# Summing activations inside the store to DRAM: a fused encoder layer on one core

## The chip, the cores and the metric

The kernel runs on one core of a Trainium2 chip. Its engines are called by their short names in the profile: PE (TensorE, the matmuls), DVE (VectorE), ACT (ScalarE), POOL (GpSimd) and SP (SyncE, which here only issues transfers). The metric is the time of one execution on the device in microseconds (us). Each engine works through its own list of instructions in order; what one needs from another it gets through semaphores.

## The reference, cut to what matters

One layer of a streaming encoder for 1056 tokens (1024 of a prompt and 32 of a sample), width 1024, hidden width 2816. After a mixing part (attention and a gated recurrence) come a feed-forward block with a short convolution and a last gated product:

```
hf = rms_norm(x, g_pre_ffn)
a, u = split(hf @ w_up, 2)                  # 1024 -> 2 x 2816
ac = b_conv + sum_j ap[:, j:j+t] * w_conv[j]        # causal, 3 taps
ffn = (gelu(ac) * u) @ w_down               # 2816 -> 1024
x = x + rms_norm(ffn, g_post_ffn)
x = x + (pe @ w_ple) * sigmoid(x @ w_ple_gate)
```

Everything is float32. The kernel multiplies each operand as a high and a low part, three PE products for one.

## The kernel before, in words

Only the last 850 us of the program matter here. They hold three stages.

**The up stage** (about 1200 to 1690 us) walks over 22 units `u`, each 128 columns of the hidden width. A unit is seven block products of Strassen's kind (`mults`, L1616 to L1618, 168 matmuls), whose results stand in three PSUM tiles X, Y, Z and are taken out by `after` (for example L1634, `nU3 = Y - s1c`, which must be done before product 5 may write into Y). Weights for the seven products are prepared some products ahead: POOL forms sums of weight blocks (L1431, L1432, L1433, L1438), ACT casts the high part (L1424), DVE subtracts for the low part (L1425). The unit's tail, `ff_tail`, runs while PE is in the next unit: convolution on ACT and DVE (L1533 to L1535), gelu on ACT (L1536), and the product with `u` on DVE (L1540, L1541), which writes the finished hidden activations `out` into one of two halves of the page `Up`.

**The down product** is again seven products `i`, over sums of activations. An even unit and the odd unit after it give the two row halves; each `out` has two column halves. With B11, B12 the halves of the even unit and B21, B22 those of the odd one, `down_parts` stores seven operands into the DRAM tiles `td[0]` to `td[6]`: B11, B11+B22, B21-B11, B22, B21+B22, B11+B12, B12-B22. Before the change the five sums are computed on chip: B11+B12 on POOL after the even unit (L1559), then after the odd unit B11+B22 on DVE (L1565), and B21-B11, B21+B22, B12-B22 on POOL (L1567, L1572, L1575; the last two are asked for by `kept["more"]` during the next unit). SP stores all seven (L1550), 264 KB each. The sums lie in the tiles `a` and `ab` of the convolution, which are free by then.

**The down stage** (about 1686 to 1932 us) reads them back: `x_in` loads a page of `td[i]` (L1708), `x_parts` splits it into high and low part (ACT L1699, DVE L1700), `w_in_` and `w_parts` load and combine w_down (L1728, L1735, L1699, L1700). For each of the seven products `i` there are 12 steps `s` (4 column blocks, each in 3 pieces of the hidden width), 24 or 18 matmuls a step (L1896 to L1898). SP issues all loads in one list. Activations for product i+1 are loaded and split during product i. `d_out` adds results into accumulators (L1767), `square` sums squares of finished ones (L1796 on ACT, L1797 on DVE).

For the norm of the first column half, `x2_norm(0)` is called in product 5: it sets a small tile `nv` to one (L1804), sums the squares over partitions with 12 one-column matmuls (L1807), and DVE makes the inverse root in 12 tiny instructions (L1808, L213 to L219). `x2_rows(0)` turns the result into rows with 12 small transposes on PE (L303). `x2_part` then applies the norm. **The gate stage** (from about 1932 us) is the last product, 2 halves `h` by 8 blocks `c` (L1987 to L1989); during half 0 the norm of the second half is made in the same way (`x2_norm(1)`, `x2_rows(1)`).

What sets the order: the program is written in the order above, but instructions that wait for nothing in the program may be put earlier in their engine's list by the scheduler that builds it. `with behind(E)` forbids that: what stands in it comes after the engine's latest instruction so far. SP and POOL each have one list, and an instruction that waits holds up all behind it there.

## Time and profile before

| | |
|---|---|
| time, median of 3 runs | 2048.68 us (2040.51 to 2050.8) |
| time of the profiled execution | 2047.88 us |
| its span, first to last instruction | 2045.9 us |
| mean granted TensorE clock | 0.989 |
| PE busy | 1987.5 us, 97% |
| DVE busy | 1498.2 us, 73% |
| ACT busy | 963.7 us, 47% |
| POOL busy | 300.9 us, 15% |

A row of the group view reads: line, engine, operation, tiles out<-in, shapes, number | busy us, mean ns of one | idle us of the engine just ahead of them and what ended it. A row of the stage view reads: stretch, its length, then for each engine busy us and in brackets the number of instructions, then the granted PE clock, the busy share of the DMA engines and GB/s. A row of the timeline has start, duration (us), engine, line and instruction; in square brackets the idle time before it and who ended it. A row of the waits has who waited, for whom, total us, times, longest. Matmuls overlap one another, so the time that PE needs is better counted in matmuls than in busy time: an undisturbed stretch of 50 us holds 416.

### The profile page before, as it was taken

The page shows a single profiled execution, that of the slowest core. Times are in us where ns is not written, and L with a number is a line of the kernel's source. Part 1 is how long each engine was busy: PE and PEld are TensorE (multiplying, and loading weights), DVE is VectorE, ACT ScalarE, POOL GpSimd, SP SyncE. Part 2 cuts the span into 40 slices and gives each one's busy share as a digit, 9 for nine tenths or more (in the row PEclk, how much of TensorE's full clock was granted, in tenths as well). Part 3 has the DMA queues.
Part 4 walks back from the last instruction along what each step waited for, and adds up shares of the span by engine and source line. Part 5 has one row for each costly group of instructions (what it writes and reads, how often), then busy time and mean ns, then how long its engine had stood idle before and what let it go on. Part 6 is the DMA issues. An engine that isn't in the chain of part 4 may idle for free. (4 is left out here: it accounts for less than half of the span.)

```text
span 2045.9 us, 38767 instructions
## 1 busy us (share of the span) xinstructions
PE 1987.5 (97%) x14858; PEld 1953.8 (95%) x14858; DVE 1498.2 (73%) x3194; ACT 963.7 (47%) x2206; POOL 300.9 (15%) x373
## 2 busy tenths in 40 slices
PE   7999999999999999999999989999999999998998
PEld 6999999999999999999999989999999998998998
DVE  6788888688888888353553868888888896777752
ACT  6555566566666666441224743333333344443432
POOL 2110100000000000012000114444554521000000
PEclk9999999999999999999999989999999999998999
DMA  8322311411111111486653552323233258897433
GB/s 261 100 88 80 110 54 61 138 42 57 57 56 56 40 53 54 137 256 188 201 163 94 179 159 79 100 86 102 81 105 100 84 175 250 241 274 228 138 108 85
DMA packets 315537, 251.71 MB, mean 123 GB/s; under 512 B 14344, under 2 KB 300571, under 8 KB 315352
## 3 DMA queue, kind: packets, MB, share of 16 engines
q1 hardware_dynamic: 308402, 227.01, 37.0%
q0 software_dynamic: 6880, 22.17, 3.2%
q8 instruction: 116, 1.90, 0.4%
q14 instruction: 69, 0.57, 0.1%
q10 hardware_dynamic: 70, 0.06, 0.0%
HBM read 180.71 MB, written 68.47 MB: 122 GB/s over the span
## 5 line engine op out<-in xcount | busy, mean ns | idle before, releaser
L1616 PE MATMUL st<-op,wt 128*128 128x264 f32 x1232 | 352.7, 286 | 19.4 <-DVE Sp L1634 16.4
L1618 PE MATMUL st<-op,wt 128*128 128x264 f32 x1232 | 351.2, 285 | 0.0
L1617 PE MATMUL st<-op,wt 128*128 128x264 f32 x1232 | 349.6, 284 | 0.0
L1616 PEld LDWEIGHTS st<-op,wt 128*128 128x128 f32 x1232 | 233.2, 189 | 24.1 <-DVE Sp L1634 20.7
L1617 PEld LDWEIGHTS st<-op,wt 128*128 128x128 f32 x1232 | 233.1, 189 | 0.0
L1618 PEld LDWEIGHTS st<-op,wt 128*128 128x128 f32 x1232 | 232.6, 189 | 0.0
L1424 ACT CAST wt<-wu 128x512 fp32r<-128x512 f32 x132 | 80.5, 619 | 210.8 <-POOL wu L1433 91.1
L1898 PE MATMUL st<-X,wd 128*128 128x264 f32 x616 | 177.6, 288 | 2.1 <-DVE wd L1700 2.1
L1896 PE MATMUL st<-X,wd 128*128 128x264 f32 x616 | 177.2, 288 | 2.4 <-ACT wd L1699 2.4
L1897 PE MATMUL st<-X,wd 128*128 128x264 f32 x616 | 176.8, 287 | 0.0
L202 PE MATMUL mm<-La,wh 128*128 128x384 f32 (+1 forms) x504 | 166.5, 331 | 0.3 <-ACT kt L342 0.3
L203 PE MATMUL mm<-Lb,wh 128*128 128x384 f32 (+1 forms) x504 | 162.5, 322 | 0.0
L204 PE MATMUL mm<-La,wl 128*128 128x384 f32 (+1 forms) x504 | 162.5, 322 | 0.0
L204 PE MATMUL mm<-Ra,wl 128*128 128x264 f32 x512 | 145.1, 284 | 1.2 <-DVE wl L186 1.2
L202 PE MATMUL mm<-Ra,wh 128*128 128x264 f32 x512 | 145.5, 284 | 0.0
L203 PE MATMUL mm<-Rb,wh 128*128 128x264 f32 x512 | 145.0, 283 | 0.0
L1425 DVE TENSOR_TENSOR wt<-wu,wt 128x512 fp32r<-128x512 f32 x132 | 116.4, 882 | 36.3 <-ACT wt L1424 36.2
L1896 PEld LDWEIGHTS st<-X,wd 128*128 128x128 f32 x616 | 118.7, 193 | 2.6 <-ACT wd L1699 2.6
L1898 PEld LDWEIGHTS st<-X,wd 128*128 128x128 f32 x616 | 118.6, 192 | 2.5 <-DVE wd L1700 2.5
L1897 PEld LDWEIGHTS st<-X,wd 128*128 128x128 f32 x616 | 118.6, 193 | 0.0
L186 DVE TENSOR_TENSOR wl<-wr,wh 128x1024 fp32r<-128x1024 f32 x64 | 78.2, 1223 | 54.8 <-ACT wh L183 53.4
L455 ACT ACTIVATE sc<-sc,st 128x257 f32<-128x257 f32 (+1 forms) x144 | 69.7, 485 | 74.9 <-DVE st L450 73.8
(468 smaller groups left out, 6056.3 us busy)
## 6 DMA issues: line engine op xcount, KB each, us to landing
wq<-in_w_down_dram SPq DMA_DIRECT2D x96, 256.0 KB
wu<-in_w_up_dram SPq DMA_DIRECT2D x44, 512.0 KB
wu<-in_w_in_dram SPq DMA_DIRECT2D x32, 512.0 KB
X<-td SPq DMA_DIRECT2D x28, 528.0 KB
wr<-in_w_in_dram SPq DMA_DIRECT2D x26, 512.0 KB
wq<-in_w_down_dram SPq DMA_DIRECT2D x48, 192.0 KB
td<-a SPq DMA_DIRECT2D x33, 264.0 KB
wr<-in_w_out_dram SPq DMA_DIRECT2D x16, 512.0 KB
```

The source lines that it names most:

```text
L186: V.tensor_tensor(lo[:], raw[:], hi[:].bitcast(F32), op=ALU.subtract)
L202: E.matmul(ps, wh, a, start=first and n == 0, stop=False)
L203: E.matmul(ps, wh, b, start=False, stop=False)
L204: E.matmul(ps, wl, a, start=False, stop=last and n == len(ks) - 1)
L1424: S.copy(t[:, 0], src)
L1425: V.tensor_tensor(t[:, 1], src, t[:, 0].bitcast(F32), op=ALU.subtract)
L1616: E.matmul(o, wh, xh, start=first and k == 0, stop=False, skip_group_check=True)
L1617: E.matmul(o, wh, xl, start=False, stop=False, skip_group_check=True)
L1618: E.matmul(o, wl, xh, start=False, stop=k == 3, skip_group_check=True)
L1896: E.matmul(o, w[:, 0, k, :], x[:, 0, k, :], start=first, stop=False)
L1897: E.matmul(o, w[:, 0, k, :], x[:, 1, k, :], start=False, stop=False)
L1898: E.matmul(o, w[:, 1, k, :], x[:, 0, k, :], start=False, stop=last)
```

## The change: what it does

Three edits.

**The sums are made by the transfers.** `down_parts` computes no sum any more. SP stores one term of each operand plainly (`to_td`), and POOL issues a transfer that adds the other term to what lies in DRAM (`add_td`, `accum_op=ALU.add`). Terms with a minus are negated by ACT first (`S.mul(neg, ..., -1.0)`, into the front of the tile `a`). For a pair of units that makes 7 plain stores from SP as before, 5 adding transfers from POOL of 264 KB each (11 pairs: 55), and 2 negations on ACT (22 in all). Gone are 44 additions on POOL and 11 on DVE. `kept["more"]` is gone with them, and the tile `ab` is no longer used for sums.

**The norm's scratch.** The memset of `nv` is held behind DVE's latest instruction.

**The column sums come later.** `x2_norm(0)` moves from step 2 to step 4 of product 5, `x2_rows(0)` from step 4 to step 8; for the second half `x2_norm(1)` moves from block 0 to block 1, `x2_rows(1)` from block 1 to 2 and the parts from blocks 2 to 5 to blocks 3 to 6.

```diff
-    def to_td(issue, i, k, src):
-        issue(td[i][k // 4][:, :, k % 4, :], src)
+    def to_td(i, k, src):
+        dma(td[i][k // 4][:, :, k % 4, :], src)
+
+    def add_td(i, k, src):
+        gdma(td[i][k // 4][:, :, k % 4, :], src, accum_op=ALU.add)
 
     def down_parts(f, a, ab, out):
 
         k, o4 = f // 2, halves(out)
-        a2 = a[:, 0:T].rearrange("p (b a c) -> p b a c", b=2, a=2)
-        b2 = ab[:, 0:T].rearrange("p (b a c) -> p b a c", b=2, a=2)
+        neg = a[:, 0:T].rearrange("p (b a c) -> p b a c", b=2, a=2)[:, 0]
+        b1, b2 = o4[:, :, 0, :], o4[:, :, 1, :]
         if f % 2 == 0:
-            to_td(dma, 0, k, o4[:, :, 0, :])
-            G.tensor_tensor(a2[:, 0], o4[:, :, 0, :], o4[:, :, 1, :], op=ALU.add)
-            to_td(dma, 5, k, a2[:, 0])
-            kept["even"] = o4
+            S.mul(neg, b1, -1.0)
+            to_td(0, k, b1)
+            to_td(1, k, b1)
+            to_td(2, k, neg)
+            to_td(5, k, b1)
+            to_td(6, k, b2)
+            add_td(5, k, b2)
             return
-        e4 = kept.pop("even")
-        to_td(dma, 3, k, o4[:, :, 1, :])
-        V.tensor_tensor(a2[:, 0], e4[:, :, 0, :], o4[:, :, 1, :], op=ALU.add)
-        to_td(dma, 1, k, a2[:, 0])
-        G.tensor_tensor(b2[:, 0], o4[:, :, 0, :], e4[:, :, 0, :], op=ALU.subtract)
-        to_td(dma, 2, k, b2[:, 0])
-
-        def more_sums(n):
-            if n == 0:
-                G.tensor_tensor(a2[:, 1], o4[:, :, 0, :], o4[:, :, 1, :], op=ALU.add)
-                to_td(dma, 4, k, a2[:, 1])
-            else:
-                G.tensor_tensor(b2[:, 1], e4[:, :, 1, :], o4[:, :, 1, :], op=ALU.subtract)
-                to_td(dma, 6, k, b2[:, 1])
-        kept["more"] = more_sums
+        S.mul(neg, b2, -1.0)
+        to_td(3, k, b2)
+        to_td(4, k, b2)
+        add_td(1, k, b2)
+        add_td(2, k, b1)
+        add_td(4, k, b1)
+        add_td(6, k, neg)
...
     def x2_norm(h):
...
-        V.memset(v[:], 1.0)
+        with behind(V):
+            V.memset(v[:], 1.0)
...
-                if i == 5 and s == 2:
+                if i == 5 and s == 4:
                     x2_norm(0)
-                if i == 5 and s == 4:
+                if i == 5 and s == 8:
                     with behind(E):
                         x2_rows(0)
...
                 if c == 0:
-                    x2_norm(1)
                     x2_load(1, 0)
                 if c == 1:
+                    x2_norm(1)
+                if c == 2:
                     with behind(E):
                         x2_rows(1)
-                if 1 < c < 6:
-                    for k in (2 * c - 4, 2 * c - 3):
+                if 2 < c < 7:
+                    for k in (2 * c - 6, 2 * c - 5):
```

How the instructions stand now. First DVE in the up stage, where the tail of an odd unit falls into the next unit: `Up` is the page of the finished activations, `Sp` the scratch that L1634 (L1632 in the changed kernel) writes, `wt` prepared weights. Before:

```order
L1540 TENSOR_TENSOR Up_15230<-a_17298,Up_15230 128x1024
L1541 TENSOR_TENSOR Up_15230<-a_17298,Up_15230 128x32
L1565 TENSOR_TENSOR a_17298<-Up_15230 128x528
L1631 TENSOR_TENSOR ab_17316<-st_17313,rbT 128x2x264
L1425 TENSOR_TENSOR wt_17499<-wu_17322,wt_17499 128x512
L1634 TENSOR_TENSOR Sp_14920<-st_17314,Sp_14920 128x528
```

and now:

```order
L1540 TENSOR_TENSOR Up_15230<-a_17310,Up_15230 128x1024
L1541 TENSOR_TENSOR Up_15230<-a_17310,Up_15230 128x32
L1629 TENSOR_TENSOR ab_17330<-st_17327,rbT 128x2x264
L1425 TENSOR_TENSOR wt_17509<-wu_17336,wt_17509 128x512
L1632 TENSOR_TENSOR Sp_14920<-st_17328,Sp_14920 128x528
```

The sum of B11 and B22 is gone; the rest keeps its order. At the same place ACT had the gelu (L1536) and three casts of the next weights:

```order
L1424 CAST wt_17471<-wu_17322 128x512
L1536 ACTIVATE a_17298<-a_17298 128x1058
L1424 CAST wt_17499<-wu_17322 128x512
L1424 CAST wt_17550<-wu_17324 128x512
L1424 CAST wt_17582<-sa_17439 128x512
```

and has now

```order
L1424 CAST wt_17481<-wu_17336 128x512
L1536 ACTIVATE a_17310<-a_17310 128x1058
L1569 ACTIVATE a_17310<-Up_15230 128x528
L1424 CAST wt_17509<-wu_17336 128x512
L1424 CAST wt_17564<-wu_17338 128x512
```

The negation (L1569, L1561 after an even unit) stands between the gelu and the casts, and reads `Up`, so it waits for DVE's L1541. POOL, from the tail of an odd unit to that of the next even one (`td_1_145` is a tile of `td[2]`, `_142` of `td[1]`, `_157` of `td[6]`, `_151` of `td[4]`, `_154` of `td[5]`), has now

```order
L1553 DMA td_1_145<-Up_15230 256x1x264
L1553 DMA td_1_142<-Up_15230 256x1x264
L1553 DMA td_1_157<-a_17310 256x1x264
L1438 TENSOR_TENSOR wu_17336<-wu_17336 128x512
L1553 DMA td_1_151<-Up_15230 256x1x264
L1431 TENSOR_TENSOR sa_17680<-wu_17569 128x512
L1432 TENSOR_TENSOR wu_17569<-wu_17567,wu_17569 128x512
L1433 TENSOR_TENSOR wu_17567<-wu_17567,sa_17680 128x512
L1599 MEMSET ab_17792 128x2
L1600 COPY ab_17792<-cach 128x2
L1438 TENSOR_TENSOR wu_17567<-wu_17567 128x512
L1553 DMA td_1_154<-Up_15230 256x1x264
```

where before the three sums L1567, L1572 and L1575 stood ahead of L1438 after the odd unit and L1559 after the even one. Three adding transfers come ahead of the weight sum L1438, one behind it, and after an even unit the one transfer comes behind L1438.

Third, DVE at the norm of the first column half in product 5 of the down stage, from the last split ahead of it (`nv`, `rsb`, `rst`, `nr` are the tiles of the inverse root, `wd` and `wq` weights, `X` activations of product 6). Before:

```order
L1700 TENSOR_TENSOR wd_22194<-wq_22077,wd_22194 128x512
L1700 TENSOR_TENSOR X_22157<-X_22157 128x1056
L1808 TENSOR_SCALAR nv_22132<-tr_22131 88x6
L1767 TENSOR_TENSOR acc_20092<-acc_20092,st_22037 128x528
L213 TENSOR_SCALAR rsb_22142<-nv_22132 128x6
L1700 TENSOR_TENSOR wd_22240<-wq_22110,wd_22240 128x384
L214 TENSOR_SCALAR rsb_22142<-rsb_22142 128x6
L1735 TENSOR_TENSOR wq_22163<-wq_22163 128x512
L217 SCALAR_TENSOR_TENSOR rst_22143<-rsb_22142 128x6
L1735 TENSOR_TENSOR wq_22198<-wq_22198 128x512
L218 TENSOR_TENSOR rst_22143<-rst_22143,nv_22132 128x6
L1700 TENSOR_TENSOR X_22192<-X_22192 128x792
```

and now:

```order
L1694 TENSOR_TENSOR X_22249<-X_22249 128x792
L1729 TENSOR_TENSOR wq_22255<-wq_22255 128x384
L1803 TENSOR_SCALAR nv_22226<-tr_22225 88x6
L213 TENSOR_SCALAR rsb_22236<-nv_22226 128x6
L214 TENSOR_SCALAR rsb_22236<-rsb_22236 128x6
L1694 TENSOR_TENSOR wd_22312<-wq_22196,wd_22312 128x512
L217 SCALAR_TENSOR_TENSOR rst_22237<-rsb_22236 128x6
L218 TENSOR_TENSOR rst_22237<-rst_22237,nv_22226 128x6
L219 SCALAR_TENSOR_TENSOR nr_22227<-rst_22237,rsb_22236 128x6
L217 SCALAR_TENSOR_TENSOR rst_22237<-nr_22227 128x6
L218 TENSOR_TENSOR rst_22237<-rst_22237,nv_22226 128x6
L219 SCALAR_TENSOR_TENSOR nr_22227<-rst_22237,nr_22227 128x6
```

The norm's instructions stood among the splits and now come nearly in one piece, behind the last split of activations for product 6 (`X_22249`). On PE the column sums stand 48 products later than before, and between them and the rows lie 84 products instead of 62. Both memsets of `nv` (L1804) stood early in the down stage, during product 0; now each stands by its norm.

More of the change, by code (lines that the diff above doesn't have):

```diff
@@ L1681, in up_unit @@
                     after(a, ps)
-                if n == 1 and "more" in kept:
-                    kept["more"](0)
-                if n == 2 and "more" in kept:
-                    kept.pop("more")(1)
                 if u == NF - 1:
@@ L1876, in layer_kernel @@
                     finish_up()
-                    for a in range(2):
-                        kept["more"](a)
                     fctx.close()
```

## The prediction

> **What bounds the kernel now.** I read the totals first, then the table by stage, to see in which stages PE stands still, then the waits of PE there, and last the timeline around each wait.
>
> ```profile
> PE 1987.5 (97%) x14858; PEld 1953.8 (95%) x14858; DVE 1498.2 (73%) x3194; ACT 963.7 (47%) x2206; POOL 300.9 (15%) x373
> 1300.00:1350.00 50.00, 48.42 (x398) 48.03 (x397) 41.41 (x52) 17.12 (x29) 23.78 (x18) 1.00 0.34 102
> 1700.00:1750.00 50.00, 45.51 (x359) 44.88 (x358) 31.29 (x47) 20.37 (x32) 9.96 (x3) 0.97 0.86 251
> 1800.00:1850.00 50.00, 50.00 (x416) 50.00 (x415) 37.48 (x55) 22.50 (x34) 0.00 (x0) 1.00 0.89 260
> 1850.00:1900.00 50.00, 43.79 (x314) 43.38 (x313) 37.08 (x65) 18.61 (x29) 0.00 (x0) 0.86 0.69 208
> PE st L1616 <- DVE Sp L1634: 14.2, 9, 1.6
> ...
> L1616 PE MATMUL st<-op,wt 128*128 128x264 f32 x1232 | 352.7, 286 | 19.4 <-DVE Sp L1634 16.4
> L1616 PEld LDWEIGHTS st<-op,wt 128*128 128x128 f32 x1232 | 233.2, 189 | 24.1 <-DVE Sp L1634 20.7
> ```
>
> PE bounds the program, so a change gains only what it takes out of PE's standstills. An undisturbed 50 us (1800 to 1850) holds 416 matmuls, 0.120 us each. The start of the down stage (1700 to 1750) holds 57 fewer: 6.9 us lost. Product 5 with its norm (1850 to 1900) holds 102 fewer: 12.3 us. In the up stage PE waited 9 times, 14.2 us in all, for L1634. These three places are those that the change touches.
>
> **The up stage: the sum that goes.** The tail of an odd unit against that of the even unit before it:
>
> ```profile
> 1419.44 1.23 DVE L1540 TENSOR_TENSOR Up<-a,Up 128x1024 f32<-128x1024 f32 x1 [0.29 <-ACT a L1536]
> 1421.30 1.48 DVE L1425 TENSOR_TENSOR wt<-wu,wt 128x512 fp32r<-128x512 f32 x1
> 1422.70 0.69 DVE L1634 TENSOR_TENSOR Sp<-st,Sp 128x528 f32<-128x528 f32 x1
> 1423.45 0.39 PE L1616 MATMUL st<-op,wt 128*128 128x264 f32 x1
> ...
> 1440.04 1.23 DVE L1540 TENSOR_TENSOR Up<-a,Up 128x1024 f32<-128x1024 f32 x1 [0.29 <-ACT a L1536]
> 1441.18 0.19 DVE L1541 TENSOR_TENSOR Up<-a,Up 128x32 f32<-128x32 f32 x1
> 1441.41 1.84 DVE L1565 TENSOR_TENSOR a<-Up 128x528 f32<-128x528 f32 x1
> 1444.90 0.70 DVE L1634 TENSOR_TENSOR Sp<-st,Sp 128x528 f32<-128x528 f32 x1
> 1445.65 0.39 PE L1616 MATMUL st<-op,wt 128*128 128x264 f32 x1 [1.58 <-DVE Sp L1634]
> ```
>
> From the start of L1540 to that of L1634 the even unit takes 3.26 us, the odd one 4.86, and only the odd one makes PE wait, 1.58 us. But in the even one too the matmul starts 0.06 us after L1634 ends (1423.39): there is no slack, and whatever else delays L1634 costs PE as much.
>
> In the changed kernel L1565 is gone, and the cast of the next weights stands behind the negation on ACT. Its price, and that of what lies around it:
>
> ```profile
> L1796 ACT ACTIVATE sq<-acc 128x528 f32<-128x528 f32 x14 | 8.9, 645 | 11.7 <-DVE acc L1767 11.6
> 1439.91 0.60 ACT L1424 CAST wt<-wu 128x512 fp32r<-128x512 f32 x1
> 1418.45 0.69 DVE L1425 TENSOR_TENSOR wt<-wu,wt 128x512 fp32r<-128x512 f32 x1 [1.22 <-ACT wt L1424]
> ```
>
> After L1540 begins, the page is ready at 1.33 us (end of L1541), the negation takes 0.65 (the nearest ACT pass over 528 columns), the cast 0.60, L1425 0.69 when POOL computes nothing beside it: L1634 starts at 3.27 us, in both kinds of unit. For odd units that is 1.59 us sooner, all of the 1.58 us wait; for even ones 0.01 us later, no change. POOL's next sum, L1438, waits for that L1425 and cannot run beside it. So the 9 waits go: 14.2 us. Bounds: if the tails of even units become shorter too, at most the 4.3 us that PE's weight loads waited beyond the matmuls come on top (20.7 against 16.4 in the last two rows of the first fence); if ACT starts its negation later by a few tenths in each of 20 units, each tenth costs 2 us. I take 14.0, nearest the rows.
>
> **What the adding transfers cost.** The trace holds none; bounds from the plain ones that POOL issues:
>
> ```profile
> L1213 POOL DMA_DIRECT2D mx_d<-ta x32 | 17.3, 542 | 593.4 <-DVE ta L1212 593.2
> L1403 POOL DMA_DIRECT2D ple_d<-ple x8 | 6.1, 756 | 25.6 <-ACT ple L1401 19.8 <-issue 5.7
> mx_d<-ta POOLq DMA_DIRECT2D x32, 132.0 KB, 3.3
> ple_d<-ple POOLq DMA_DIRECT2D x8, 528.0 KB, 6.3
> ```
>
> 264 KB lies between: 0.54 to 0.76 us of POOL, 3.3 to 6.3 us to land, more if reading the target counts. Three issues (about 1.9 us) replace three sums (at least 1.3 us each) ahead of L1438, so POOL is sooner than now; the fourth waits for a store to land, behind L1438, when POOL has nothing to do before the next L1431. Nothing reads a sum before the down stage, and an `Up` half is rewritten some 25 us after it is finished. So I take nothing for them here; the upper bound is the first rival. [...]
>
> **The start of the down stage.**
>
> ```profile
> 1699.87 7.53 POOL L1567 TENSOR_TENSOR ab<-Up 128x528 f32<-128x528 f32 x1 [21.55 <-DMA wq<-in_w_down_dram]
> 1697.33 1.26 SPq L1728 DMA_DIRECT2D wq<-in_w_down_dram  x1
> SPq L1550 <- POOL ab L1567: 6.9, 1, 6.9
> 1711.29 0.56 SPq L1728 DMA_DIRECT2D wq<-in_w_down_dram  x1
> 1714.26 0.10 DVE L1804 MEMSET nv<- 128x6 f32 x2 [8.06 <-DMA td<-ab]
> 1720.00:1725.00 5.00, 4.28 (x22) 4.06 (x23) 3.91 (x7) 2.86 (x6) 0.00 (x0) 0.70 1.00 247
> ```
>
> The last odd unit's sum on POOL takes 7.53 us beside DVE's splits; SP waits 6.9 us for it with the weight loads of w_down behind; then the memset of `nv`, whose memory was `ab`, holds DVE 8.06 us until the store has landed, with the splits of weights behind it. PE runs dry and its clock falls to 0.70. All three go: no sum, no store from `ab`, no memset here. What is late next is SP's load of activations of product 1, last piece, which needs an added operand: finished page, two issues on POOL, landing, some 5 to 8 us after L1541. Weights are issued ahead of that load, where now SP issues none for 12.7 us (1698.6 to 1711.3), and they are fetched six steps (about 16 us) before their use. I take 6.5 of the 6.9 us; bounds 3 and 6.9.
>
> **The norm in product 5.**
>
> ```profile
> 1864.11 0.70 DVE L1797 TENSOR_TENSOR sqd<-sqd,sq 128x528 f32<-128x528 f32 x1
> 1864.86 1.53 PE L1807 MATMUL tr<-ones,sqd 128*88 128x1 f32 x12 [4.08 <-DVE sqd L1797]
> 1865.00:1870.00 5.00, 5.00 (x29) 5.00 (x30) 4.98 (x8) 3.17 (x4) 0.00 (x0) 0.53 0.87 269
> 1876.62 0.98 DVE L1700 TENSOR_TENSOR X<-X 128x792 fp32r<-128x792 f32 x1
> 1878.80 2.72 PE L303 MATMUL tr<-ident,nr 88*128 88x88 f32 x12 [2.13 <-DVE nr L219]
> 1924.11 0.70 DVE L226 TENSOR_TENSOR x<-acc,x 128x528 fp32r<-128x528 f32 x1
> 1880.00:1885.00 5.00, 5.00 (x25) 5.00 (x25) 3.03 (x5) 0.76 (x2) 0.00 (x0) 0.50 0.63 177
> ```
>
> PE came to the sums at 1860.78 and waited 4.08 us, then 2.13 us for the rows; the clock fell to 0.53 and 0.50 after them. 48 products later is 5.8 us later: 1866.6, and the squares are done at 1864.81. That wait goes, with 1.8 us to spare. The rows come 1.5 us of sums and 84 products (10.1 us) after that, at 1878.2. DVE's root now stands behind the last split for product 6, which ended at 1877.60, perhaps 0.7 sooner without the small instructions ahead of it; then one combination of weights (0.56), one split (0.69), one addition (0.70) and 12 small instructions at 0.2: ready at about 1881. PE waits some 2.9 us again, and with the clock at half for 5 us as in the last row loses 2.5 more. 12.3 less 5.4 makes 6.9 us. Bounds: 12.3, if activations land sooner, and 2, if the applied norm, which DVE finishes at 1924.8 now (last row of L226), 7 us before the gate stage, is what PE, some 9 us earlier there, waits for next.
>
> [...]
>
> **The gate stage.**
>
> ```profile
> 1935.00:1940.00 5.00, 4.49 (x41) 4.30 (x40) 2.78 (x5) 2.35 (x6) 0.00 (x0) 1.00 0.26 76
> ```
>
> The wait of the second column sums, 0.5 us, goes: a block later their squares are done. The parts end a block later (block 6) and have block 7 as cover, 6.5 us; without it each late microsecond would be PE's.
>
> **The sum**: 14.0 + 6.5 + 6.9 + 0.5 = 27.9 us. From the profiled execution's 2047.88 us: 2020 us; that execution is 0.8 us below the median of the runs.
>
> **Rivals.**
>
> *Adding transfers delay the weights (slower).* Place: the loads of `wu`, from which POOL begins its sums.
>
> ```profile
> 1449.80 1.59 SPq L1413 DMA_DIRECT2D wu<-in_w_up_dram  x2
> 1454.72 1.29 POOL L1431 TENSOR_TENSOR sa<-wu 128x512 f32<-128x512 f32 x1 [5.70 <-DMA wu<-in_w_up_dram]
> ```
>
> Here L1431 began as its weights landed, 4.9 us after the issue; from it the chain runs through L1433, a cast, the gelu and L1540 to L1634, which has no slack. One adding transfer runs near each pair of loads. Each microsecond that it delays them costs 20 units 20 us: from 1.4 us on nothing is left of the gain, from 1.9 us the kernel is clearly slower. With 3 us (half of the 6.3 us of the nearest large transfer): 2020 + 60 = 2080. Against it: the DMA engines are busy 0.34 of this stage. Chance 0.08.
>
> *The negation keeps L1634 late.* ACT is in order; 0.5 us later than I worked out in 20 units leaves 14 - 10 = 4 us of the up stage: 2030. For it: no slack at all. Against it: ACT is busy 17 of 50 us. 0.15.
>
> *The later stalls move instead of going.* SP is held by the landing as long as by the sum, and PE waits for the applied norm: 6.5 falls to 0 and 6.9 to 2, 2031. That is also the case that the edits of the norm don't do what they say. 0.12.
>
> **How the numbers follow.** Forecast 2020 (its own range 2012 to 2026) 0.6; the two middle rivals 0.27; slower 0.08; others near no change 0.05. What a measurement can tell from no change is about 0.5%, 10 us: all that ends below 2038 is faster, 0.86; same 0.07; slower 0.07. The range: below, all of 14.2 + 4.3 + 6.9 + 12.3 + 0.5 = 38 us gained, 2010, and 2 for the spread of runs: 2008; above, 2038, which takes in both middle rivals.
>
> **What would show it.** Right: no wait of PE for the successor of L1634 above 0.3 us, about 411 matmuls in 50 us of the up stage (398 and 1.58 us at 0.12); over 400 in the first 50 us of the down stage; no wait at the column sums, one of 2 to 3 us at the rows. Wrong: POOL's weight sums waiting for `wu`, ACT's casts waiting behind the negation, SP waiting for an adding transfer more than 8 us, or PE idle ahead of the gate stage.

## The result: 1.1% faster, some three quarters of the forecast gain, and not by the instruction that was named

The changed kernel takes 2024.06 us at the median against 2046.77 us before on the same chip: a ratio of 0.9894, 95% interval 0.9863 to 0.9926. The forecast was 2020 us, 27.9 us less than before; the ratio gives 21.7 us. Its profiled execution took 2028.1 us (span 2026.1), 19.8 us less than the profiled one before.

The table by stage at the places whose rows the prediction showed, of the changed kernel (after the window: busy us and count of PE, PEld, DVE, ACT, POOL; granted clock, DMA share, GB/s):

```profile
1300.00:1350.00 50.00, 49.78 (x410) 49.57 (x410) 39.53 (x51) 18.21 (x31) 25.92 (x21) 1.00 0.57 130
1700.00:1750.00 50.00, 48.46 (x393) 47.63 (x393) 33.81 (x47) 25.89 (x40) 0.00 (x0) 1.00 0.96 296
1800.00:1850.00 50.00, 48.65 (x397) 48.02 (x396) 33.63 (x51) 18.90 (x29) 0.00 (x0) 1.00 0.82 242
1850.00:1900.00 50.00, 45.28 (x343) 44.86 (x342) 40.30 (x71) 22.36 (x37) 0.00 (x0) 0.90 0.75 218
```

The up stage went from 398 matmuls to 410, the start of the down stage from 359 to 393, product 5 from 314 to 343. The stretch from 1800 to 1850 us, full before at 416, lost 19.

PE's waits for VectorE in the up stage (us in total, times, longest), where L1632 is the former L1634 and L1627 the former L1629:

```profile
PE st L1614 <- DVE Sp L1627: 2.0, 1, 2.0
PE st L1614 <- DVE Sp L1632: 0.2, 1, 0.2
```

The nine waits of 1.6 us are gone. The tail of an odd unit, by the timeline, shows why L1632 is in time, and what it now stands behind:

```profile
1433.66 1.23 DVE L1540 TENSOR_TENSOR Up<-a,Up 128x1024 f32<-128x1024 f32 x1 [0.30 <-ACT a L1536]
1434.80 0.18 DVE L1541 TENSOR_TENSOR Up<-a,Up 128x32 f32<-128x32 f32 x1
1435.08 0.65 ACT L1569 ACTIVATE a<-Up 128x528 f32<-128x528 f32 x1 [1.45 <-DVE Up L1541]
1435.63 1.13 ACT L1424 CAST wt<-wu 128x512 fp32r<-128x512 f32 x2
1436.26 0.69 DVE L1425 TENSOR_TENSOR wt<-wu,wt 128x512 fp32r<-128x512 f32 x1 [0.66 <-ACT wt L1424]
1436.87 0.70 DVE L1632 TENSOR_TENSOR Sp<-st,Sp 128x528 f32<-128x528 f32 x1
```

From L1540 to L1632 are 3.21 us (4.86 before), on the path that the prediction drew: the negation 0.65 us, the cast, L1425 at 0.69.

To set the kernels side by side, PE's matmuls in five stretches of each profiled execution. A matmul is 0.12 us; the stretches are the up stage, the start of the down stage, products 2 to 4, product 5, and product 6 with the gate stage. The last column is the ratio of the times to those of the kernel before.

| kernel | 1250–1650 | 1650–1750 | 1750–1850 | 1850–1900 | 1900–2000 | ratio, 95% |
|---|---|---|---|---|---|---|
| before | 3150 | 755 | 829 | 314 | 828 | 1 |
| changed | 3250 | 804 | 810 | 343 | 835 | 0.9894 (0.9863–0.9926) |
| norm edits only | 3139 | 771 | 828 | 362 | 835 | 0.9974 (0.9956–0.9992) |
| sums only | 3251 | 796 | 753 | 371 | 835 | 0.9923 (0.9901–0.9945) |
| one sum | 3057 | 761 | 819 | 317 | 833 | 1.0071 (1.0048–1.0094) |
| sum on VectorE | 3252 | 811 | 798 | 345 | 835 | 0.9883 (0.9859–0.9908) |
| idle sums on POOL | 2911 | 740 | 828 | 404 | 771 | 1.0119 (1.0087–1.0151) |
| negated twice | 3164 | 775 | 808 | 350 | 835 | 0.9936 (0.9911–0.9961) |
| plain stores | 3260 | 829 | 812 | 351 | 835 | 0.9866 (0.9840–0.9893) |
| norm later | 3264 | 797 | 792 | 421 | 824 | 0.9868 (0.9846–0.9891) |
| and loads spread | 3252 | 800 | 804 | 421 | 805 | 0.9872 (0.9846–0.9897) |
| and piece late | 3249 | 804 | 791 | 416 | 818 | 0.9867 (0.9847–0.9888) |
| and piece on POOL | 3263 | 785 | 800 | 421 | 811 | 0.9886 (0.9870–0.9903) |
| norm later, piece late, sum on VectorE | 3266 | 818 | 796 | 421 | 820 | 0.9836 (0.9814–0.9858) |

Changed against before: +100, +49, -19, +29, +7, together 166 matmuls or 19.9 us, which is the 19.8 of the two executions (at 1250 us they are level, with 8669 matmuls before and 8663 now). A kernel that is early is further along at the same microsecond, so the stretches behind 1750 us compare only roughly between kernels that differ much (the norm of "sums only" lies partly in its third column, that of the idle sums in the fifth). The first 300 us, whose code is the same in all, hold 1862 to 1916 matmuls from one execution to the next, up to 6.5 us, and at 1250 us the executions lie up to 87 matmuls apart: that is why the counts behind 1250 us say more of small effects than the times.

### The profile page after: what moved, and what is told of

Its sections match the earlier page's. It is cut to its first block, busy times and chain, and to the rows that moved or that the text cites. A ratio compares the mean times of both kernels' runs of the same rounds, so it can differ in the third digit from the quotient of the medians.

```text
span 2026.1 us, 38830 instructions
## 1 busy us (share of the span) xinstructions
PE 1988.8 (98%) x14858; PEld 1955.4 (97%) x14858; DVE 1468.4 (72%) x3183; ACT 974.2 (48%) x2228; POOL 284.0 (14%) x384
## 3 DMA queue, kind: packets, MB, share of 16 engines
q0 software_dynamic: 21840, 37.05, 8.6%
## 4 chain that ended last, share of the span: by engine, by line
PE 62%; issue 8%; DMA 8%; DVE 7%; POOL 7%; ACT 3%; SPq 1%; POOLq 0%; DVEq 0%; ACTq 0%
PE mm L202 7%; PE mm L203 7%; PE mm L204 7%; DMA td<-Up 4%; PE st L1891 2%; PE st L1889 2%; PE st L1890 2%; POOL wu L1433 2%; POOL wu L1432 2%; DMA X<-td 2%; PE st L1980 2%; PE st L1982 2%; PE st L1981 2%; PE G L841 2%; PE Y L838 2%
## 5 line engine op out<-in xcount | busy, mean ns | idle before, releaser
L1425 DVE TENSOR_TENSOR wt<-wu,wt 128x512 fp32r<-128x512 f32 x132 | 107.8, 817 | 47.7 <-ACT wt L1424 47.6
L1891 PEld LDWEIGHTS st<-X,wd 128*128 128x128 f32 x616 | 116.9, 190 | 3.0 <-DVE wd L1694 3.0
L1889 PEld LDWEIGHTS st<-X,wd 128*128 128x128 f32 x616 | 117.1, 190 | 1.6 <-ACT wd L1693 1.6
L1890 PEld LDWEIGHTS st<-X,wd 128*128 128x128 f32 x616 | 117.1, 190 | 0.0
```

Source lines behind the costliest of these rows:

```text
L1425: V.tensor_tensor(t[:, 1], src, t[:, 0].bitcast(F32), op=ALU.subtract)
L1889: E.matmul(o, w[:, 0, k, :], x[:, 0, k, :], start=first, stop=False)
L1890: E.matmul(o, w[:, 0, k, :], x[:, 1, k, :], start=False, stop=False)
L1891: E.matmul(o, w[:, 1, k, :], x[:, 0, k, :], start=False, stop=last)
```

## The experiments

### Each half of the change alone

Kernel before, with the norm's edits alone:

```
+        with behind(V): V.memset(v[:], 1.0)
-  i == 5: x2_norm(0) at s == 2, x2_rows(0) at s == 4
+  i == 5: x2_norm(0) at s == 4, x2_rows(0) at s == 8     (and x2_norm(1), x2_rows(1) one block later)
```

> The kernel before with only the three edits of the norm: memset of nv behind VectorE's earlier work, column sums and rows of both halves issued later. My theory (each part acts in its own place): the up stage is as before (398 matmuls in 50 us, PE waits 1.58 us in odd units for L1634), the norm in product 5 gains about 3.5 us as it did in the changed kernel, the memset's stall of 8.06 us of VectorE at 1714 us goes and gives 1 to 3 us, the gate stage 0.5: 5 to 7 us less than before, ratio about 0.997. Rival (the adding transfers are what makes the later places of the norm useful, or SP's blocked queue alone sets the start of the down stage): 0 to 4 us less.

Changed kernel, with those edits undone:

> The changed kernel with the three edits of the norm undone (memset in its old place, column sums and rows early): only the sums go by adding transfers and ScalarE negates. My theory: up stage as in the changed kernel (410 to 413 matmuls in 50 us), start of the down stage about 4 us better than before, norm as before (314 matmuls between the marks that held 343): 16 to 18 us less than before, ratio about 0.992. Rival (the memset's place and the late norm carry the gain after the up stage, and the adding transfers cost as much behind the up stage as they gain): 10 to 13 us less, ratio about 0.994.

Measured: 5.3 us less (0.9974) and 15.7 us less (0.9923). Together 21.0, against 21.7 for the whole change: by the times the two halves add, about as the first theory had it in both. The intervals (1.6 to 9.0 us and 11.2 to 20.2 us) don't exclude the rivals by themselves. By the counts behind 1250 us the halves alone gain 59 and 130 matmuls, 23 more than the two together; 19 of these are the norm in product 5, which gains 48 alone and 29 in the changed kernel. The norm's edits leave the waits in the up stage as they were. At the start of the down stage they bring only 5 matmuls, 0.6 us (446 from 1690 to 1750 us, 441 before), where 1 to 3 us were expected. The other 11 of the second column are missing in the first: this execution is 62 matmuls ahead at 1250 us, so that a stall which the kernel before has at 1653 us falls ahead of 1650 us here. The memset no longer holds VectorE, but SP and PE wait there as before (waits of PE, then of SP, with the norm's edits alone):

```profile
PE st L1897 <- ACT wd L1699: 4.3, 1, 4.3
...
SPq L1550 <- POOL ab L1567: 6.9, 1, 6.9
```

Without the memset's edit, "sums only" loses 33 matmuls between 1650 and 1750 us (796 of the 829 that a full stretch holds), where the kernel before loses 57 from 1700 to 1750 us alone. Its memset waits for nothing, since nothing is stored from `ab` any more. So POOL's late sum, and the store behind it, were the stall that counted there.

### Which sum was it? L1565 on VectorE, or POOL's sums beside it

Kernel before, with L1565 alone gone, POOL's four sums kept:

```
+            to_td(dma, 1, k, o4[:, :, 0, :])                                          (even unit)
-        V.tensor_tensor(a2[:, 0], e4[:, :, 0, :], o4[:, :, 1, :], op=ALU.add)         (odd unit, L1565)
-        to_td(dma, 1, k, a2[:, 0])
+        gdma(td[1][k // 4][:, :, k % 4, :], o4[:, :, 1, :], accum_op=ALU.add)
```

> The kernel before with one sum changed: only VectorE's L1565 goes (product 1's activations: a store in the even unit, one adding transfer in the odd one); POOL keeps its four sums, ScalarE negates nothing. My theory (L1565 ahead of L1634 on VectorE is the whole wait): L1634's wait falls from 14 us to under 1, some 410 matmuls in 50 us, 12 to 14 us less than before: ratio about 0.9935. Rival (POOL's sums beside VectorE's passes also lengthen the chain to L1634): half of it, 6 to 7 us, ratio 0.997, with waits of 0.5 to 1 us left.

Measured: 1.0071, 14.5 us slower than before. Both theories had it faster. PE's waits in the up stage, and one odd tail by the timeline (line numbers as in the kernel before; L1572 and L1575 are two of POOL's sums, L1438 its weight sum):

```profile
PE st L1616 <- DVE Up L1636: 17.0, 10, 1.7
PE st L1616 <- DVE Sp L1629: 8.9, 9, 1.0
PE st L1616 <- DVE Sp L1634: 2.0, 2, 1.4
```

```profile
1442.60 0.69 DVE L1634 TENSOR_TENSOR Sp<-st,Sp 128x528 f32<-128x528 f32 x1
1443.22 4.34 DVE L1425 TENSOR_TENSOR wt<-wu,wt 128x512 fp32r<-128x512 f32 x1
1447.48 0.69 DVE L1636 TENSOR_TENSOR Up<-Sp,st 128x528 f32<-128x528 f32 x1
...
1442.71 1.77 POOL L1572 TENSOR_TENSOR a<-Up 128x528 f32<-128x528 f32 x1
1443.99 1.78 POOL L1575 TENSOR_TENSOR ab<-Up 128x528 f32<-128x528 f32 x1
1445.27 1.72 POOL L1438 TENSOR_TENSOR wu<-wu 128x512 f32<-128x512 f32 x1
```

L1634 is in time now, but the split L1425 behind it takes 4.34 us instead of 0.69: it ends at 1447.56, 0.57 us after the last of POOL's three passes (1446.99), as if it had only then begun. The stall moved from L1634 to the next result that PE needs, L1636, and became longer. This run also puts an adding transfer between POOL's sums, which moves L1572 some 0.6 us later against L1540; how much of the longer stall is owed to that, no run separates.

In the kernel before, L1565 itself stood beside POOL's sums (the prediction's row has it from 1441.41 to 1443.25 us), and so did the split behind it:

```profile
1441.35 1.34 POOL L1567 TENSOR_TENSOR ab<-Up 128x528 f32<-128x528 f32 x1 [2.98 <-DVE Up L1540]
1442.64 1.78 POOL L1572 TENSOR_TENSOR a<-Up 128x528 f32<-128x528 f32 x1
...
1443.79 1.19 DVE L1425 TENSOR_TENSOR wt<-wu,wt 128x512 fp32r<-128x512 f32 x1
```

L1565 ends 0.56 us after POOL's L1567, and L1425 0.56 us after L1572. L1565 takes 1.84 us for work that takes 0.71 alone (next run), L1425 1.19 for 0.69: 1.13 and 0.50 us too long, 1.63 in all. The whole tail is 1.64 us longer than in the next run, which has the same sum on VectorE and none on POOL (4.86 us against 3.22).

Changed kernel, with VectorE's sum back and POOL summing nothing:

```
-            to_td(1, k, b1)
+            kept["b1"] = b1
-        add_td(1, k, b2)
+        V.tensor_tensor(s1, kept.pop("b1"), b2, op=ALU.add)     (s1: the free half of a)
+        to_td(1, k, s1)
```

> The changed kernel with VectorE's sum for product 1 back (L1565's work and a plain store in odd units); POOL still sums nothing, ScalarE still negates. Theory P (after the run with one sum changed: POOL's sums beside VectorE's passes, not L1565, are the wait): the sum takes 0.70 us instead of 1.85 and lies mostly in the 0.66 us that VectorE waits for ScalarE's cast there; waits of PE under 0.2 us a unit, at most 3 us slower than the changed kernel, ratio to before 0.990 to 0.991. Theory L (the prediction: L1565 itself is the wait): 0.7 to 1.6 us in each of 10 odd units, 7 to 15 us slower than the changed kernel, ratio 0.993 to 0.997.

Measured: 0.9883, the same as the changed kernel; 3252 matmuls in the up stage against 3250. An odd tail (L1573 is the sum, L1634 the changed kernel's L1632):

```profile
1432.02 1.22 DVE L1540 TENSOR_TENSOR Up<-a,Up 128x1024 f32<-128x1024 f32 x1 [0.30 <-ACT a L1536]
1433.16 0.18 DVE L1541 TENSOR_TENSOR Up<-a,Up 128x32 f32<-128x32 f32 x1
1433.38 0.71 DVE L1573 TENSOR_TENSOR a<-Up 128x528 f32<-128x528 f32 x1
1434.01 0.70 DVE L1631 TENSOR_TENSOR ab<-st,rbT 128x528 f32<-128x528 f32 x1
1434.63 0.69 DVE L1425 TENSOR_TENSOR wt<-wu,wt 128x512 fp32r<-128x512 f32 x1
1435.24 0.70 DVE L1634 TENSOR_TENSOR Sp<-st,Sp 128x528 f32<-128x528 f32 x1
```

The sum fits into the time in which VectorE waits for ScalarE's cast (0.66 us in the changed kernel). From the start of L1540 to that of L1634 are 3.22 us, with the sum in between (3.21 in the changed kernel): it costs nothing. Theory P holds, theory L, which was the prediction's, does not.

Changed kernel, with POOL computing sums that nothing reads:

```
+            G.tensor_tensor(d2[:, 0], b1, b2, op=ALU.add)       (even; d2 lies in ab)
+        G.tensor_tensor(d2[:, 0], e1, b2, op=ALU.add)           (odd, three of them)
+        G.tensor_tensor(d2[:, 1], b1, e1, op=ALU.add)
+        G.tensor_tensor(d2[:, 0], b1, b2, op=ALU.add)
```

> The changed kernel, and POOL computes sums as in the kernel before (one in even units, three in odd ones), into memory that nothing reads: results, transfers and ScalarE's negations are the changed kernel's. Theory P (POOL's sums beside VectorE's passes are what made PE wait): the waits at the tails of odd units come back, 1.5 to 2.5 us in each of 10 units, VectorE's splits L1425 grow from a mean of 0.82 us to 1.0 or more, 15 us or more slower than the changed kernel, ratio to before 0.997 or above. Theory L (VectorE's own sum was the wait): the same as the changed kernel within 3 us.

Measured: 1.0119, 24 us slower than before and 46 us slower than the changed kernel; 339 matmuls fewer in the up stage. PE's waits there, and one odd tail (L1639 is the changed kernel's L1632, L1632 its copy L1625 on ScalarE):

```profile
PE st L1621 <- ACT Sp L1632: 23.9, 9, 3.9
PE st L1621 <- DVE Sp L1639: 11.3, 10, 1.2
```

```profile
1447.78 1.87 DVE L1425 TENSOR_TENSOR wt<-wu,wt 128x512 fp32r<-128x512 f32 x1 [0.66 <-ACT wt L1424]
1449.57 0.69 DVE L1639 TENSOR_TENSOR Sp<-st,Sp 128x528 f32<-128x528 f32 x1
1450.18 2.67 DVE L1425 TENSOR_TENSOR wt<-wu,wt 128x512 fp32r<-128x512 f32 x1
...
1446.47 1.34 POOL L1575 TENSOR_TENSOR ab<-Up 128x528 f32<-128x528 f32 x1 [2.98 <-DVE Up L1540]
1447.76 1.33 POOL L1574 TENSOR_TENSOR ab<-Up 128x528 f32<-128x528 f32 x1
```

The splits are long again (1.87 and 2.67 us), with nothing changed but POOL's work. The dose is larger than in the kernel before, though: besides 11.3 us for L1639, PE waits 23.9 us for ScalarE's copy, and POOL, whose sums here stand ahead of its transfers and weight sums, waits 41.4 us for `wu` (5.7 in the kernel before). The sign is shown by this run; the size in the kernel before is not, and rests on the rows of its tail above.

### Is there slack behind the negation?

Changed kernel, each negation done twice:

```
             S.mul(neg, b1, -1.0)
+            S.mul(neg, b1, -1.0)          (and the same for b2 in odd units)
```

> The changed kernel with each negation on ScalarE done twice. Theory (no slack: whatever delays the cast behind the negation delays L1632, and PE waits for it): about 0.55 us in each of 21 units, 11 us slower than the changed kernel, ratio to before about 0.995, PE's wait for L1632 near 0.5 us a unit. Rival (a few tenths to half a microsecond of slack are there since the waits are gone): at most 3 us slower, no wait above 0.2 us.

Measured: 0.9936, 8.6 us slower than the changed kernel by the ratios; 86 matmuls fewer in the up stage, 10.3 us. There is no slack to speak of. But the wait shows elsewhere than expected (lines two further on than in the changed kernel: L1629 is its L1627, L1636 its L1634; for L1634, its L1632, PE waits once, 1.7 us):

```profile
PE st L1616 <- DVE Sp L1629: 7.9, 8, 1.0
PE st L1616 <- DVE Up L1636: 2.0, 9, 0.3
```

VectorE's chain is late as a whole, and PE pays at whichever result comes last.

### What adding costs in the transfer

Changed kernel, with `accum_op` left out of POOL's transfers, so that the second term overwrites the first and the sums are left out:

> The changed kernel with plain stores by POOL in place of the adding ones: the second operand overwrites the first, so the sums are left out; issues, bytes written and queues are the same. Theory (adding costs only in the transfer: it lands later and loads the DMA engines more): landing falls from 5.8 us to 3.5 to 4.5, the DMA share of the up stage from 0.57 to about 0.45, SP's wait of 5 us for the added operand shortens by 1 to 2 us; time within 3 us of the changed kernel, ratio to before 0.988 to 0.990. Rival (the adding itself starves the start of the down stage): 5 us or more faster than the changed kernel, ratio under 0.987.

Measured: 0.9866. By the counts behind 1250 us (the five columns summed) it gains 45 matmuls over the changed kernel, 6087 against 6042, 5.4 us; 25 of them, 3.0 us, at the start of the down stage, which is full. The page's DMA parts, first of the changed kernel, then with plain stores (packets, MB, share; KB each, median us from issue to landing):

```profile
q0 software_dynamic: 21840, 37.05, 8.6%
...
td<-Up POOLq DMA_DIRECT2D x44, 264.0 KB, 5.8
```

```profile
q0 software_dynamic: 11280, 37.05, 5.4%
...
td<-Up POOLq DMA_DIRECT2D x44, 264.0 KB, 3.4
```

For the same 37.05 MB the queue of the adding transfers counts 21840 packets instead of 11280, about twice as many, and an adding transfer lands in 5.8 us instead of 3.4. The DMA engines' share of the up stage falls from 0.58 to 0.42 (windows from 1250 to 1650 us). Up to 1600 us all of that is hidden (410 matmuls from 1300 to 1350 us against 411 with plain stores, 413 in both from 1550 to 1600 us). At the start of the down stage, where the share is 0.99 (0.95 with plain stores, both from 1650 to 1750 us), it is not. The theory, which put the time at no more than 3 us, is wrong by its own signs: the rival's came out, 5.4 us by the counts and a ratio under 0.987, though only 3.0 us of them lie at the start of the down stage, and the interval overlaps that of the changed kernel. With plain stores SP waits 1.5 us for the last added operand instead of 5.0, VectorE's L1729 2.1 us for its weights instead of 4.6, and the stretch holds its full 829 matmuls. So the adding costs the start of the down stage what was still lost there.

Two runs ask how. In both the norm is later, as in the next part, and SP's wait of some 5 us for the last added operand, with weights queued behind it, is the suspect. The piece is loaded three steps later:

```
+                at = (0, 1, 2, 3, 7, 8) if i == 0 else range(6)     (steps at which product i + 1's pieces are loaded)
```

> The kernel with the norm later, and the last piece of product 1's activations (the one that waits for the last added operand) is loaded at steps 7 and 8 of product 0 instead of 4 and 5, and split three steps behind. Theory (at the start of the down stage the loss is SP's wait of about 5 us for that operand, with loads of weights behind it, and ScalarE's of 7.6 us, with casts of weights behind it): SP waits under 0.5 us, the windows from 1690 to 1705 us hold 44 matmuls each instead of 44, 22 and 38: 3 us faster than with the norm later alone, ratio to before about 0.985. Rival (the DMA engines, busy 1.1 there, bring the weights late whatever waits): the same count of matmuls, same time.

or POOL issues it:

```
+        (gdma if (i, j) == (1, 2) else dma)(t[:, 1, 0:n, :].bitcast(F32), td[i][j][:, p, 0:n, :])
```

> The kernel with the norm later, and the two loads of the last piece of product 1's activations issued by POOL, behind the adding transfers that it issues there, instead of by SP. SP then waits for no added operand, and the bytes and the adding transfers are the same. Theory S (what is left of the loss at the start of the down stage is SP's wait of 4.8 us, with the loads of weights behind it): the two windows from 1650 to 1750 us, 394 and 405 matmuls with the norm later alone, sum to 815 or more, 2 us faster than it. Theory D (the adding transfers themselves load the DMA engines, busy 1.1 there, so that the weights land late): the sum stays at 795 to 808, same time; VectorE's L1729 waits 4 us for wq as before.

The first changed little: SP came to the load only some 3 us later and still waited 3.9 us (under 0.5 was expected), 1690 to 1705 us held 112 matmuls for 104, and the time stayed the same. In the second SP waits for no operand at all, and the stretch holds 785 matmuls, 12 fewer than with the norm later alone and below what either theory had; the clock fell to 0.66 from 1700 to 1705 us. The timeline there:

```profile
1691.68 0.56 DVE L1729 TENSOR_TENSOR wq<-wq 128x384 f32<-128x384 f32 x1 [4.61 <-DMA wq<-in_w_down_dram]
...
1697.63 0.85 ACT L1693 CAST X<-X 128x792 fp32r<-128x792 f32 x1 [4.79 <-DMA X<-td]
```

The weights land as late as ever with SP free (4.6 us of waiting; 4.4 with the norm later alone), so SP's wait is not the cause. That the adding transfers crowd the weights out of the DMA engines (busy 1.07 from 1650 to 1700 us with the norm later alone, 0.97 with plain stores) is what remains, an inference, with ScalarE's wait for X, behind which casts of weights stand, as a second way that no run separated.

### The norm still later

Changed kernel:

```
-  i == 5: x2_norm(0) at s == 4, x2_rows(0) at s == 8
+  i == 5: x2_norm(0) at s == 6, x2_rows(0) at s == 11
```

> The changed kernel with the first column sums two steps later (s 6 for 4) and the rows three steps later (s 11 for 8) in product 5. My theory: the waits of 1.2 us (sums) and 3.5 us (rows) and the low clock behind them are the 8.8 us still lost there, and nothing follows that is short of the later norm: 6 to 9 us less than the changed kernel, no gap of PE above 0.5 us at the sums or the rows, clock 1.00 from 1850 to 1900 us. Rival (late activations and weights, with the DMA engines busy 0.95 there, are the cause, or the applied norm becomes late for the gate stage): at most 2 us less, gaps of PE then for X, wd or the gate stage's first operand.

Measured: 0.9868. The two waits are gone (421 matmuls for 343), and a part is given back next door, where the changed kernel has 397 (a window of this run):

```profile
1800.00:1850.00 50.00, 47.00 (x379) 45.95 (x378) 34.92 (x52) 20.85 (x31) 0.00 (x0) 1.00 0.86 255
```

Behind 1250 us it has 56 matmuls more than the changed kernel, 6.7 us; by the ratios 5 us, with intervals that overlap. What is lost between 1805 and 1820 us was put down to bursts of loads, and tried by spreading them:

```
+    X_AT = (0, 1, 3, 4, 6, 7)        (steps at which the six pieces of the next product are loaded)
```

> The kernel with the norm later (the run before last named so) and, beside it, the six loads of activations of the next product issued at steps 0, 1, 3, 4, 6, 7 of a product instead of 0 to 5, and split three steps behind as before. Theory (what is still lost between 1690 and 1850 us comes from bursts of loads, with the DMA engines busy 1.0 and weights landing behind the activations): the windows from 1700 to 1850 us, which hold 405, 415 and 379 matmuls there, rise to 410 or more, 3 to 6 us faster than with the norm later alone, ratio to before about 0.984. Rival (the engines' orders, not the bursts: VectorE's splits then come later, or the bytes are simply too many): within 2 us of it, 0.986 to 0.988.

Measured: 0.9872, no difference: the third stretch holds 804 for 792, the last 805 for 824. The bursts are not the cause, or not alone. Nor is it the adding: with plain stores 1800 to 1850 us hold 398. What it is stays open.

The three edits that helped or did no harm, together:

> The changed kernel with three edits: the norm later, the last piece of product 1 later, and product 1's sum on VectorE with a plain store. Theory (each acts in its own place): norm 7 us, start of the down stage 3 us, VectorE's sum 0 to 2 us by fewer adding transfers: 8 to 11 us faster than the changed kernel, 2012 to 2016 us against 2045, ratio to before 0.984 to 0.985. Rival (what is won at one place is lost at the next, as between 1805 and 1820 us): 0.987 as with the norm later alone.

Measured: 2012.17 us at the median, 0.9836 (0.9814 to 0.9858), 79 matmuls or 9.5 us ahead of the changed kernel behind 1250 us. This version beats the kernel before and the changed one; of the norm later alone it is 23 matmuls, 2.8 us, ahead, with intervals that overlap.

## Why the prediction was right, point by point

**The up stage: 14.0 us forecast.** The stretch from 1250 to 1650 us gained 100 matmuls, 12.0 us, and that from 1650 to 1690 us 17 (316 before, 333 now): 14.0 us. That it is the forecast to the decimal is chance. The tails gained more, 15 matmuls in 50 us (413 for 398), and a stall in the unit near 1635 us, which no term had, took 32 matmuls or 3.8 us back (1600 to 1650 us hold 381 for 413). The size and the path (negation, cast, L1425, L1632) are right. The step that failed is "In the changed kernel L1565 is gone": L1565 did go, but so did POOL's sums, and the working gives the gain to the wrong one. Without L1565 but with POOL's sums the kernel is slower than before; with L1565's work but without POOL's sums it is as fast as the changed one. The condition that decides stood in the working as a clause of L1425's price, "when POOL computes nothing beside it", and was not priced: the 1.84 us of L1565 and the 1.48 us of an L1425 were rows with POOL's passes beside them. "Whatever else delays L1634 costs PE as much" is right in size (a second negation cost 10.3 us by the counts); the rival of a late negation did not happen, but was as near as that.

**The price of the adding transfers.** "I take nothing for them" holds in the up stage only. A landing of 5.8 us lies inside the bounds of 3.3 to 6.3. POOL's issue, estimated at 0.54 to 0.76 us, is 1.08 us long where it stands alone (at 1441.59 us), but three in a row held POOL for 1.9 us, as worked out (from 1435.18 us to the start of L1438 at 1437.11). The clause "more if reading the target counts" was the right warning; what it missed is the start of the down stage, where the share of the DMA engines is 0.99 (1650 to 1750 us). The slower rival, late `wu`, did not happen: POOL's L1431 never waited for `wu` in the changed kernel, and L1433 once, for 1.0 us.

**The start of the down stage: 6.5 of 6.9 us forecast.** The stretch from 1650 to 1750 us gained 49 matmuls, but 17 of them lie ahead of 1690 us, in the last units of the up stage. From 1690 to 1750 us it is 33 (474 for 441), 4.0 us: inside the bounds of 3 and 6.9, and 2.5 us short of the forecast. The 3.0 us that are still lost are those that plain stores win back. The expected late load was there, SP's wait of 5.0 us for the added operand. The rows, of the waits of SP and of the timeline:

```profile
SPq L1702 <- DMA td<-Up: 5.0, 1, 5.0
```

```profile
1698.52 0.56 DVE L1729 TENSOR_TENSOR wq<-wq 128x384 f32<-128x384 f32 x1 [4.64 <-DMA wq<-in_w_down_dram]
1702.13 0.85 ACT L1693 CAST X<-X 128x792 fp32r<-128x792 f32 x1 [7.59 <-DMA X<-td]
```

The step that was off is "Weights are issued ahead of that load": they were, and landed late all the same. Of the three things that "go", the memset gave little by itself (0.6 us for all that the norm's edits do there).

**The norm in product 5: 6.9 us forecast, 3.5 gained** (29 matmuls). The waits of PE:

```profile
PE tr L303 <- DVE nr L219: 3.5, 1, 3.5
...
PE tr L1802 <- DVE sqd L1791: 1.2, 1, 1.2
```

The rows waited 3.5 us where 2.9 were worked out. The sums, which were to be ready "with 1.8 us to spare", came 1.2 us late: ScalarE's square stood behind a split of X that waited 2.93 us for its load. With the norm's edits alone, without the adding transfers, the sums did not wait, the rows waited 3.8 us, and the stretch gained 48 matmuls, 5.8 us. So the mechanism is right, and the term was mis-sized by what the other half of the change moved there.

**The gate stage: 0.5 us forecast**, 7 matmuls or 0.8 us gained, and PE was never idle ahead of it.

**What no term had**: the unit near 1635 us and the loss at 1815 to 1825 us, 3.8 and some 2.3 us. The first is not new: in the same unit PE waited 1.2 us for L1629 before (at 1653 us, behind the counted stretch) and waits 2.0 us for its successor L1627 now, with the clock falling behind it. Two sums of down weights stand there on VectorE ahead of the unit's convolution. Before, and now with POOL's weight sums beside them:

```profile
1645.59 0.69 DVE L1735 TENSOR_TENSOR wq<-wq 128x512 f32<-128x512 f32 x1
1646.88 1.29 DVE L1735 TENSOR_TENSOR wq<-wq 128x384 f32<-128x384 f32 x1 [0.61 <-DMA wq<-in_w_down_dram]
...
1631.45 3.04 DVE L1729 TENSOR_TENSOR wq<-wq 128x512 f32<-128x512 f32 x2 [1.16 <-DMA wq<-in_w_down_dram]
...
1632.45 1.62 POOL L1432 TENSOR_TENSOR wu<-wu,wu 128x512 f32<-128x512 f32 x1
1634.15 1.48 POOL L1433 TENSOR_TENSOR wu<-wu,sa 128x512 f32<-128x512 f32 x1
```

The first sum now waits for its weights, and the pair then takes 3.04 us beside POOL's passes, as L1425 and L1565 were long beside POOL's sums in the tails (1.19 us for 0.69, 1.84 for 0.71). With plain stores PE waits for L1627 at most 1.2 us at a time; that late weights are the reason is argued from these rows, not shown by a run of its own. The cause of the second loss stays open.

Together: 14.0 + 4.0 + 3.5 + 0.8 - 2.3 = 20.0 us of the 27.9 forecast. Of the signs that were named beforehand two failed, "no wait at the column sums" (1.2 us) and "over 400 in the first 50 us of the down stage" (391).

## What to carry to other kernels

Before an instruction is blamed for a wait, compare its duration with that of the same shape elsewhere: 1.84 us against 0.71 said that a neighbour on another engine was the cost, and removing the victim alone made the kernel 14.5 us slower. Moving the sums to the DMA engines paid here though it moved more bytes: the up stage gained 12.0 us while their share rose from 0.31 to 0.58 and their rate from 94 to 132 GB/s (1250 to 1650 us), and 3.0 us were lost to the adding at the start of the down stage, where the share is 0.99. So look up the busy share at every stage that the work reaches, not only at the one that gains. And two edits that each look local can meet (the later norm gained 48 matmuls in product 5 alone and 29 beside the adding transfers, where a split of X waited 2.93 us for its load): price them alone, and then the later one again with the first in place.

## What the runs showed of the hardware

L1425 and L1565, passes of VectorE with both operands in the main on-chip memory (SBUF), were long beside POOL's sums and ended 0.56 to 0.57 us after POOL's pass in the odd tails of the kernel before and of the run with one sum changed: L1565 took 1.84 us beside POOL's L1567 and 0.71 without POOL's sums, L1425 4.34 us beside three passes of POOL in a row and 0.69 alone. L1634, `Sp<-st,Sp`, which reads one operand from PE's result memory (PSUM, `st`), was not: in the run with one sum changed it takes 0.69 us at 1442.60 us, while POOL's L1572 runs (from 1442.71 us), and it takes 0.69 to 0.70 us in every row above. Why the two kinds of pass differ, no run asked.

The clock did not follow the length of a gap alone. The same wait of 2.0 us for L1627 near 1635 us left the clock at 1.00 in the kernel with the norm later (in each 5 us from 1630 to 1645 us), while in the changed one it was down to 0.50 from 1640 to 1642.5 us. At the sums, where a gap of 1.2 us is followed by 1.1 us of one-column matmuls, it was down to 0.50 from 1855 to 1857.5 us:

```profile
1640.00:1642.50 2.50, 2.50 (x14) 2.50 (x13) 1.84 (x4) 1.16 (x2) 1.71 (x3) 0.50 0.28 94
1855.00:1857.50 2.50, 2.50 (x14) 2.50 (x13) 2.50 (x4) 1.59 (x2) 0.00 (x0) 0.50 0.90 257
```

How much idle time lowers the clock, and why a gap of 2.0 us did so in one execution and not in the other, no run shows. In the sum of the prediction, the 2.5 us taken for the clock at the rows was right to be there: behind the wait of 3.5 us it was 0.50 from 1870 to 1872.5 us and 0.58 up to 1875 us.
